# Residual gate's products placed in attention and in the branch projection, one PSUM pool from the groups on, and the forms' buffers opened before the keys

## The chip, the cores and the metric

The kernel runs on one core of a Trainium2 chip. The metric is device time in microseconds (us) of one execution; each figure is the median of several runs. PE is the matrix engine (PEld its weight loads), DVE the vector engine, ACT the scalar engine (activation functions, copies), POOL the GpSimd engine, SP the engine that does nothing here but start loads. SP, ACT and POOL start transfers; all transfers share the core's 16 DMA engines.

## The reference, cut to what matters

```python
# SEQ=512 tokens, D=2048, CTX=256, 12 query heads on 4 key heads of 128, FNet width 512
shift, scale, gate = split(silu(c) @ w_ada + b_ada, 3)         # modulation; gate is a row of 2048
h  = rmsnorm(x, norm_g) * (1 + scale) + shift
hc = rmsnorm(ctx, norm_g) * (1 + scale_c) + shift_c
kc, vc = heads(hc @ w_in[:, K and V]);  kc = rmsnorm(kc)
p  = h @ w_in                                                   # q, k, v, z_a, u_b, z_b, g_a, g_b
q, k = rope(rmsnorm(q)), rope(rmsnorm(k))
attn = softmax(q @ [k; kc].T) @ [v; vc]
y_a  = (attn * silu(z_a)) @ w_pa
y_b  = (real(fft2(u_b per group)) * silu(z_b)) @ w_pb
y    = (sigmoid(g_a) * y_a + sigmoid(g_b) * y_b) @ w_out
out  = rmsnorm(x + gate * y, final_g)
```

The *residual gate* is the row `gate`: a product of `silu(c)` with 2048 columns of `w_ada`. It is wanted only at the very end, where the output is scaled.

## The kernel before

Matmuls are made in pairs of numbers: each fp32 operand is split into a high and a low part (`split_from`: ACT rounds the high part, L141, DVE takes the difference for the low part, L142), and `mm3` issues three matmuls, high by high, high by low, low by high (L268, L269, L270). So every weight piece of 128x1024 that comes in by DMA costs ACT about 1.05 us and DVE about 1.22 us before PE can use it.

The program goes through these stages; Python loops write them out, and a scheduler then sets the order of the instructions on each engine, by priorities and by when it expects operands. The order on an engine is fixed afterwards: an instruction that waits holds all behind it on that engine, the DMA issues of that engine included.

- Start (0 to about 205 us): modulation, the pieces `u_b` for the FNet, and the FNet itself. `form_row(j)` builds row j of the operand combinations ("forms" S3, Z5, S2, S4 ..., since the big projection is a Strassen-Winograd product of 2x2 blocks) and stores it to a scratch tensor `f_d` in HBM; POOL issues this store (L558). The tile `f` has one buffer, so the next row's first write (L551) waits for the store.
- Keys and values (about 205 to 315 us), weights `w_kv`, then seven groups of about 81 us: groups 0 to 2 give q and z (stored to `qz_d`), groups 3 to 6 give the sigmoid gates g_a, g_b (`gate_done`, stored to `g_d` by ACT). A group runs Strassen pieces P2 ... Q5, P7, Q3, Q4; each has weight pieces `wr<-in_w_g` loaded by SP, and accumulates in PSUM tiles `x` and `y`. The forms come back from `f_d` by SP (`s<-f_d`, L313) into tiles of the pool `fm` and are split on arrival.
- Attention (about 895 to 1097 us): 48 steps (12 heads x 4 row blocks), in each step `scores(i)` (matmuls, DVE maximum L1068, ACT Exp), `turn(i-1)` (PE transposes of the weights, split into `pth` and `ptl`), every second step `values`, and between them a `filler`: the matmuls of w_pb. PSUM has a pool of its own here (`psa`).
- Branch projection (about 1097 to 1230 us): four column blocks (`CHUNKS`) x six pieces of w_pa (`wr<-in_w_pab`), 24 matmuls each, in another PSUM pool; POOL loads `g_d` back (`s<-g_d`), DVE multiplies by the gates (L1215, L1219, L1220), PE transposes the merged rows, ACT copies them out (L1162).
- Output groups (about 1230 to 1395 us), weights w_o, then the final norm. `load_rows` (issued by ACT, L1240) reads the gate row back from the scratch tensor `gs`.

The residual gate before: in groups 3 to 6 a list of jobs asks for one piece of the transposed w_ada (`ask_gate(q)`, 512 KB, SP, `wr<-in_w_gate`) and two jobs later DVE multiplies it by the row silu(c) and sums along the row (`use_gate`, L955, result in `gparts[:, q]`). There are 32 pieces; the row silu(c) is loaded and made twice (`crow`: L941 ACT, L942 DVE), one half for 16 pieces. The pieces use the same raw buffers `wr` as the weights. After group 6 DVE adds the parts (L1011, L1012: `gcol`, 128x16) and POOL stores them to `gs` (L1013) in 4-byte pieces.

Of the kernel before, what the change touches and what calls it, by code (L numbers as in the profile page):

```python
# [93 lines left out]
def block_kernel(ctx, tc, xT, ctxT, x, c_row, w_ss, w_gate, vecs, qkg, rope, dft_c, dft_s,  # L94
# [223 lines left out]
    def tiles(key):  # L318

        new = [take((1024,), F32R, fm) for _ in range(2)]  # L320
        kept.setdefault(key, []).extend(new)
        return new
# [223 lines left out]
    def form_row(j):  # L546

        f = pap.tile([P, 4, 256], F32, tag="f4", bufs=1, name=uid("f4"))
        v = pap.tile([P, 2, 256], F32, tag="f2", bufs=1, name=uid("f2"))
        for kb, t in ((j, f[:, 0:2, :]), (j + 8, v)):  # L550
            nc.vector.tensor_tensor(t, *(w[kb].bitcast(F32).rearrange("p (i c) -> p i c", i=2) for w in (hhi, hlo)),  # L551
                                    op=ALU.add)
# [4 lines left out]
        nc.vector.tensor_tensor(s4, v[:, 0, :], s2, op=ALU.subtract)  # L557
        nc.gpsimd.dma_start(f_d[:, :, j, :].rearrange("f p c -> p f c"), f)  # L558

    work = start_work()  # L560
    done = 0
    for kb in range(KK):
# [20 lines left out]
    form_row(6)  # L583
    form_row(7)
    pa.close()
# [89 lines left out]
    chain += [rp.tile([P, 1024], F32, name=f"R{pc}") for pc in range(4)]  # L675
    raw_pools.append((rp, 2, "raw", 2))
    cp, cpp = region("cp", "right")
# [88 lines left out]
    pss.close()  # L766
    fm = ctx.enter_context(tc.tile_pool(name="fm", bufs=1, reuse_waits="tile"))
# [4 lines left out]
    psum = [psp]  # L772
    rows4 = lambda hi, lo: [(hi[:, j, :], lo[:, j, :]) for j in range(4)]

    def split_form(src, pool):
        hi, lo = slot(pool, (4, 256), F32R), slot(pool, (4, 256), F32R)
        split_from(src, hi, lo)
        return rows4(hi, lo)

    def pair(tag):  # L780
        return psum[-1].tile([P, 2, 512], F32, tag=tag, bufs=2, name=uid(tag))

# [11 lines left out]
    class Banks:  # L794


        def __init__(self):
            self.b = [pair("y") for _ in range(2)]

# [79 lines left out]


    for i, f in enumerate(FORMS):
        forms[f] = [None] * 8
        for h in range(2):
            if (i, h) < (3, 1):
                whole[f, h] = slot(fm, (4, 256))

    ropeq = qzp.tile([P, 2, 4, HD], F32, name="ropeq")
# [45 lines left out]

    crow = None

    def silu_of_row(half):

        row = gvp.tile([P, 1024], F32, tag="crow", bufs=1, name=uid("crow"))
        nc.scalar.dma_start(row, c_row[:, 1024 * half : 1024 * half + 1024].broadcast_to([P, 1024]))
        e = flat(new_ev())  # L940
        nc.scalar.activation(e, row, ACT.Tanh, scale=0.5)  # L941
        nc.vector.scalar_tensor_tensor(row, e, 1.0, row, op0=ALU.add, op1=ALU.mult)  # L942
        return row

# [4 lines left out]
    def use_gate(q):  # L949

        if not any(e.key == ("gate", q) for e in ahead):
            jobs.insert(0, lambda: use_gate(q))
            return
        w = get_aside(("gate", q))
        nc.vector.scalar_tensor_tensor(w, w, 0.5, crow, op0=ALU.mult, op1=ALU.mult, accum_out=gparts[:, q : q + 1])  # L955

    def finish_jobs():
        for _ in range(16):
            load_more()
            job()  # L960
        assert not jobs

# [17 lines left out]
    for g in range(NQZ + NGATE):  # L980
        if g == NQZ:
            qzs.close()
            gvs, gvp = region("gvp", "right", reuse_waits="tile")
            raw_pools.append((gvp, 1, "raw", 1))
        if g in (NQZ, NQZ + 2):
            finish_jobs()
            crow = silu_of_row((g - NQZ) // 2)
            for q in range(8 * (g - NQZ), 8 * (g - NQZ) + KK):
                jobs += [lambda q=q: ask_gate(q), lambda: None, lambda q=q: use_gate(q)]
        group = Group(g, forms, new_ev, qz_done if g < NQZ else gate_done, {"a": "x", "b": "y", "c": "x"})  # L990
        for name in ONE_GROUP:
# [4 lines left out]
            if (g, name) == (0, "Q5"):  # L996
                hl_pools += range(MORE_HL)
                rotations()
            elif (g, name) == (LAST, "Q3"):
                finish_jobs()  # L1000
                raw_pools.pop()

                free += [(fm, f"s{i % KK}") for i in range(7, 7 + KK)]
# [8 lines left out]
    nc.vector.tensor_tensor(gcol, gcol, bada[:, 2 * KK :], op=ALU.add)  # L1012
    nc.gpsimd.dma_start(gs.rearrange("k p -> p k"), gcol)  # L1013
    gvs.close()
    evs.close()
    psg.close()

# [3 lines left out]
    ats_, atp = region("atp", "right", reuse_waits="tile")  # L1021
    psa_, psa = region("psa", None, space=PSUM, reuse_waits="tile")
    b1 = lambda: psa.tile([P, 512], F32, tag="b1", bufs=1, name=uid("pb"))
    ybs, S = {}, {}

    def filler():
# [5 lines left out]
        for n, j in enumerate(CHUNKS):  # L1032
            w = [get(("pab", j, pc)) for pc in BRANCH_B]
            for t in range(4):
                if t % 2 == 0:

                    y = chain[2 * n + t // 2].rearrange("p (t c) -> p t c", t=2) if n < 2 else take((2, 512))
                    ybs[j, t // 2] = y
                acc = psa.tile([P, 512], F32, tag="acc", bufs=1, name=uid("pf"))
                s = slice(t * P, t * P + P)  # L1040
# [18 lines left out]
    def scores(i):  # L1059
# [3 lines left out]
        qh, ql = qs[h][:, 0, s], qs[h][:, 1, s]  # L1063
        sc = psa.tile([P, 1024], F32, tag="sc", bufs=2, name=uid("sc"))
        for a, b in ((0, 512), (512, 768)):
# [12 lines left out]
    def turn(i):  # L1078
        p = probs.pop(i)
        tp = psa.tile([P, 1024], F32, tag="tp", bufs=1, name=uid("tp"))  # L1080
        for k in range(KT):
# [7 lines left out]
    def values(half):  # L1089
# [13 lines left out]
        if second:  # L1103
# [4 lines left out]
            if h % GQ == GQ - 1:  # L1108
                give(*kept.pop(h // GQ))

    filled = 0
# [21 lines left out]
    fill(1)  # L1133
    ats_.close()
    psa_.close()
    psum.append(ctx.enter_context(tc.tile_pool(name="psm", bufs=1, space=PSUM, reuse_waits="tile")))

# [4 lines left out]
    def load_gate(which, half, j):  # L1142
        t = take((2, 512), pool=gp)
        nc.gpsimd.dma_start(t, g_d[which, half, j].rearrange("p (t c) -> p t c", t=2))
        return t

    raws, merged, mf, comb = {}, {}, {n: [None] * 8 for n in ("A11", "A12", "A22") + FORMS}, {}
    held = {}
# [44 lines left out]
    for n, j in enumerate(CHUNKS):  # L1193
# [7 lines left out]
        ga = [load_gate(0, h, j) for h in range(2)]  # L1201
        accs = [pair("yx"[n % 2]) for _ in range(2)]
        for pc in BRANCH_A:
            wh, wl = get(("pab", j, pc))
            sh, sl = S[pc]
            for t in range(4):
                s = slice(t * P, (t + 1) * P)
                for k in range(2):
                    mm3(accs[t // 2][:, t % 2, :], sh[:, k, s], sl[:, k, s], wh[:, k, :], wl[:, k, :],
                        pc == 0 and k == 0, pc == BRANCH_A[-1] and k == 1)  # L1210
            if pc:
                job()
            if pc in (2, 3):
                y = ybs[j, pc - 2]
                nc.vector.tensor_tensor(y, gb[pc - 2], y, op=ALU.mult)  # L1215
                give(gb[pc - 2])
                gb[pc - 2] = y
        for h in range(2):
# [3 lines left out]
        give(*ga)  # L1222
        turned = [lambda j=j, i=i, n=n: turn_merged(j, i, "yx"[n % 2]) for i in range(2)]
        if n == 3:
# [151 lines left out]
    hl_pools.append(more)  # L1376
    out_group = Group(8, mf, new_o, lambda half, c, v, t: out_done(half, 2 + c, v, t), {"a": "y", "b": "x", "c": "y"})
    for name in OUT_GROUP:
        out_group.run(name)

    last_group = Group(9, mf, new_o, out_done, {"a": "y", "b": "x", "c": "y"}, last)
    for name in ONE_GROUP:
# [91 lines left out]
```

## Time and the profile before

| what | value |
|---|---|
| median of 3 runs | 1409.72 us (1404.27, 1409.72, 1410.72) |
| profiled execution | 1406.93 us, span 1405.2 us |
| PE busy | 1338.1 us, 95% |
| DVE busy | 981.5 us, 70% |
| ACT busy | 672.7 us, 48% |
| POOL busy | 142.3 us, 10% |
| moved | 265.73 MB read from HBM, 27.27 MB written |
| largest weight streams | `wr<-in_w_g` 112 loads, `wr<-in_w_gate` 32, `wr<-in_w_pab` 32, 512 KB each |

How to read it: PE does nearly all of the span, so time can come only from PE's idle stretches, from the stretches in which PE's clock was granted at half (the column PEclk of the windows view is the mean granted clock; 0.90 over 35 us means 3.5 us of full-speed work lost), or from fewer matmuls. A row of a group reads: line, engine, operation, written tile <- read tiles, shapes, count, then busy us and mean ns of one, then the engine's idle time just before these instructions and what ended it.

### The profile page before, as it was taken

Reading aid. Unit: us, or ns where it says so; the run is one execution under the profiler, and the core shown is the slowest. Engines: PE = TensorE matmul, PEld = TensorE weight load, DVE = VectorE, ACT = ScalarE, POOL = GpSimd, SP = SyncE. Lnnn points to the kernel's source line nnn. Section 1 sums busy time; section 2 is a strip of 40 time slices with the busy share of each in tenths; the row PEclk is TensorE's granted clock in tenths of the full one; section 3 lists DMA queues with packets and bytes.
Section 4 is the critical chain, followed back from the end, with each engine's and each line's share of the span. In section 5 each row is a group of like instructions: output and inputs, shape, how many; then the busy total and the mean of one; then the engine's idle time right before and its main releaser. Section 6 shows DMA issues by size and latency. Waiting matters only on the chain. (4 is left out here: it accounts for less than half of the span.)

```text
span 1405.2 us, 17732 instructions
## 1 busy us (share of the span) xinstructions
PE 1338.1 (95%) x6664; PEld 1084.1 (77%) x6664; DVE 981.5 (70%) x1266; ACT 672.7 (48%) x1036; POOL 142.3 (10%) x196
## 2 busy tenths in 40 slices
PE   7999899999999999999999996999999999999996
PEld 4667688787888888787777875888888788887885
DVE  4778695767887878786676864666766355578777
ACT  5322163446555555444354442677666223354544
POOL 1111000112111111101000010000000100010100
PEclk9999999999999999999999998999999999999998
DMA  9898466559888888897889998420311654378983
GB/s 384 341 371 313 150 229 211 183 180 319 236 226 217 200 245 210 242 349 214 260 258 247 302 253 192 154 87 26 96 46 35 220 180 135 106 153 217 229 224 135
DMA packets 90085, 294.16 MB, mean 209 GB/s; under 512 B 9232, under 2 KB 22032, under 8 KB 85648
## 3 DMA queue, kind: packets, MB, share of 16 engines
q1 hardware_dynamic: 51264, 178.46, 38.1%
q0 software_dynamic: 22320, 95.44, 27.0%
q10 hardware_dynamic: 16416, 19.14, 4.1%
q8 instruction: 52, 0.85, 0.2%
q14 instruction: 33, 0.27, 0.1%
HBM read 265.73 MB, written 27.27 MB: 209 GB/s over the span
## 5 line engine op out<-in xcount | busy, mean ns | idle before, releaser
L141 ACT ACTIVATE whi<-wr 128x1024 fp32r<-128x1024 f32 (+1 forms) x151 | 158.0, 1047 | 261.7 <-PE y L270 89.2
L142 DVE TENSOR_TENSOR wlo<-wr,whi 128x1024 fp32r<-128x1024 f32 (+1 forms) x151 | 181.4, 1206 | 100.2 <-ACT whi L141 99.8
L269 PE MATMUL x<-wlo,s 128*128 128x512 f32 x448 | 177.8, 397 | 8.2 <-DVE wlo L142 8.2
L268 PE MATMUL x<-whi,s 128*128 128x512 f32 x448 | 177.8, 397 | 4.5 <-ACT ev L837 3.4
L270 PE MATMUL x<-whi,s 128*128 128x512 f32 x448 | 176.5, 394 | 0.0
L268 PE MATMUL y<-whi,s 128*128 128x512 f32 x404 | 160.4, 397 | 10.5 <-ACT whi L141 7.3
L269 PE MATMUL y<-wlo,s 128*128 128x512 f32 x404 | 160.5, 397 | 6.1 <-DVE wlo L142 6.0
L270 PE MATMUL y<-whi,s 128*128 128x512 f32 x404 | 159.5, 395 | 0.0
L141 ACT ACTIVATE whi<-R 128x1024 fp32r<-128x1024 f32 x96 | 100.9, 1058 | 105.4 <-PE x L270 59.8
L142 DVE TENSOR_TENSOR wlo<-R,whi 128x1024 fp32r<-128x1024 f32 x96 | 116.5, 1220 | 22.2 <-ACT whi L141 22.0
L269 PEld LDWEIGHTS x<-wlo,s 128*128 128x128 f32 x448 | 85.8, 192 | 28.4 <-DVE wlo L142 10.8
L268 PEld LDWEIGHTS x<-whi,s 128*128 128x128 f32 x448 | 85.5, 191 | 23.3 <-ACT ev L837 3.8
L270 PEld LDWEIGHTS x<-whi,s 128*128 128x128 f32 x448 | 85.8, 192 | 18.0
L268 PEld LDWEIGHTS y<-whi,s 128*128 128x128 f32 x404 | 77.1, 191 | 27.8 <-ACT whi L141 7.7
L269 PEld LDWEIGHTS y<-wlo,s 128*128 128x128 f32 x404 | 77.1, 191 | 25.5 <-DVE wlo L142 9.8
L224 POOL DMA_DIRECT2D R<-in_w_g x56 | 48.8, 872 | 435.5 <-DVE wlo L142 263.7
L270 PEld LDWEIGHTS y<-whi,s 128*128 128x128 f32 x404 | 77.1, 191 | 16.7 <-DVE s L142 0.8
L141 ACT ACTIVATE s<-wr 128x512 fp32r<-128x512 f32 (+2 forms) x82 | 55.1, 690 | 55.7 <-DMA wr<-b_d 12.9
L215 DVE TENSOR_TENSOR wr<-R,wr 128x1024 f32<-128x1024 f32 x36 | 43.9, 1221 | 46.5 <-DMA wr<-in_w_g 28.3
L269 PE MATMUL x<-s,s 128*128 128x512 f32 x192 | 74.7, 389 | 0.0
L270 PE MATMUL x<-s,s 128*128 128x512 f32 x192 | 74.7, 389 | 0.0
L141 ACT ACTIVATE s<-R 128x512 fp32r<-128x512 f32 (+1 forms) x89 | 57.4, 661 | 30.8 <-PE x L270 17.4
(299 smaller groups left out, 2892.9 us busy)
## 6 DMA issues: line engine op xcount, KB each, us to landing
wr<-in_w_g SPq DMA_DIRECT2D x112, 512.0 KB, 4.8
wa<-in_w_ss POOLq DMA_DIRECT2D x28, 1024.0 KB, 9.0
R<-in_w_g POOLq DMA_DIRECT2D x56, 512.0 KB, 8.3
wr<-in_w_gate SPq DMA_DIRECT2D x32, 512.0 KB, 4.7
wr<-in_w_pab SPq DMA_DIRECT2D x32, 512.0 KB, 3.9
R<-in_w_g SPq DMA_DIRECT2D x28, 512.0 KB, 5.3
wr<-in_w_kv SPq DMA_DIRECT2D x24, 512.0 KB, 4.0
wr<-in_w_o SPq DMA_DIRECT2D x24, 512.0 KB, 5.1
```

Source lines behind the costliest of these rows:

```text
L141: nc.scalar.activation(hi, src, ACT.Copy)
L142: return nc.vector.tensor_tensor(lo, src, hi.bitcast(F32), op=ALU.subtract)
L215: nc.vector.tensor_tensor(src, chain[e.pc], src, op=ALU.subtract)
L224: nc.gpsimd.dma_start(chain[e.pc], e.nxt, accum_op=ALU.add)
L268: nc.tensor.matmul(o, ah, bh, start=start, stop=False, skip_group_check=cont)
L269: nc.tensor.matmul(o, ah, bl, start=False, stop=False, skip_group_check=cont)
L270: nc.tensor.matmul(o, al, bh, start=False, stop=stop, skip_group_check=cont)
```

## The change

Nothing of what is computed changes, and the counts of matmuls, of loads and of the gate's 32 products are the same. It has these parts:

1. The store of a form row goes from POOL to ACT (`keep_row`), and is written one block later, before the next row is built.
2. The pool `fm` is opened before the keys, so the six first form loads have free buffers there; the later forms take slots from `fm` and a second pool `fm2`.
3. In groups 3 to 6 no gate pieces are loaded or multiplied any more.
4. In attention, every third step uses one gate piece and asks for the next (16 in all); in the branch projection one piece per step of `m` (16 more); only then are `gcol` and its store to `gs` issued. `crow` now lies in a buffer of the pool `rp` (`raw1`).
5. PSUM has one pool (`psp`, tags x, y0, y1) from the groups to the end; attention's tiles `sc`, `tp`, `acc`, `b1` are taken from it. The first six pieces of the branch projection (`products`, a generator) start in attention's last three steps, and the filler runs three pieces further ahead.

```diff
-        nc.gpsimd.dma_start(f_d[:, :, j, :].rearrange("f p c -> p f c"), f)
+        made.append((j, f))
+    def keep_row():
+        j, f = made.pop()
+        nc.scalar.dma_start(f_d[:, :, j, :].rearrange("f p c -> p f c"), f)
...
+        if kb > 10:
+            keep_row()
         if kb >= 10:
             form_row(kb - 10)
...
+    fm = ctx.enter_context(tc.tile_pool(name="fm", bufs=1, reuse_waits="tile"))
+    for i, f in enumerate(FORMS):
+        for h in range(2):
+            if (i, h) < (3, 1):
+                whole[f, h] = slot(fm, (4, 256))
...
-    psg, psp = region("psg", None, space=PSUM, reuse_waits="tile")
+    psp = ctx.enter_context(tc.tile_pool(name="psp", bufs=1, space=PSUM, reuse_waits="tile"))
...
     def use_gate(q):
         w = get_aside(("gate", q))
-        nc.vector.scalar_tensor_tensor(w, w, 0.5, crow, op0=ALU.mult, op1=ALU.mult, accum_out=gparts[:, q : q + 1])
+        nc.vector.scalar_tensor_tensor(w, w, 0.5, crow[0], op0=ALU.mult, op1=ALU.mult, accum_out=gparts[:, q : q + 1])
...
-        if g in (NQZ, NQZ + 2):
-            finish_jobs()
-            crow = silu_of_row((g - NQZ) // 2)
-            for q in range(8 * (g - NQZ), 8 * (g - NQZ) + KK):
-                jobs += [lambda q=q: ask_gate(q), lambda: None, lambda q=q: use_gate(q)]
...
-    nc.vector.tensor_tensor(gcol, gparts[:, :KK], gparts[:, KK:], op=ALU.add)
-    nc.vector.tensor_tensor(gcol, gcol, bada[:, 2 * KK :], op=ALU.add)
-    nc.gpsimd.dma_start(gs.rearrange("k p -> p k"), gcol)
...
     for i in range(NSTEP + 2):
...
+            if i == 4:
+                silu_of_row()
...
-        want = 60 * (i + 1) // NSTEP if i < NSTEP else 64
+        want = min(3 + 61 * (i + 1) // NSTEP, 64)
...
+        if i % 3 == 2 and i < NSTEP:
+            if i > 2:
+                use_gate(i // 3 - 1)
+            ask_gate(i // 3)
...
+        if i == NSTEP - 1:
+            fill(1)
+            first_sums = [pair("x") for _ in range(2)]
+            first = products(CHUNKS[0], first_sums)
+        if i >= NSTEP - 1:
+            next(first)
+            next(first)
+    use_gate(KK - 1)
+    load_row(1)
+    silu_of_row()
...
+            m += 1
+            if 3 <= m < 19:
+                use_gate(KK + m - 3)
+            if m < 16:
+                ask_gate(KK + m)
+            if m == 19:
+                nc.vector.tensor_tensor(gcol, gparts[:, :KK], gparts[:, KK:], op=ALU.add)
+                nc.vector.tensor_tensor(gcol, gcol, bada[:, 2 * KK :], op=ALU.add)
+                nc.gpsimd.dma_start(gs.rearrange("k p -> p k"), gcol)
```

The scheduler turns this into the following orders (rows: line, operation, written tile <- read tiles; numbers behind a name tell buffers apart).

SP before, at the end of the keys' weights: the six form loads stand behind nine loads of the first group's weights.

```order
L177 DMA wr_2922<-in_w_g 128x1024
L177 DMA wr_3103<-in_w_g 128x1024
L177 DMA wr_2940<-in_w_g 128x1024
L313 DMA s_2787<-f_d 128x1024
L313 DMA s_2788<-f_d 128x1024
L313 DMA s_2789<-f_d 128x1024
L313 DMA s_2790<-f_d 128x1024
L313 DMA s_2791<-f_d 128x1024
L313 DMA s_2792<-f_d 128x1024
L177 DMA wr_2999<-in_w_g 128x1024
```

And SP after, at the beginning of the keys' weights:

```order
L706 DMA ct_2261<-in_ctxT 128x512
L313 DMA s_2024<-f_d 128x1024
L706 DMA ct_2295<-in_ctxT 128x512
L177 DMA wr_2338<-in_w_kv 128x1024
L313 DMA s_2025<-f_d 128x1024
L313 DMA s_2026<-f_d 128x1024
L177 DMA wr_2362<-in_w_kv 128x1024
L313 DMA s_2027<-f_d 128x1024
L177 DMA wr_2407<-in_w_kv 128x1024
L313 DMA s_2028<-f_d 128x1024
L313 DMA s_2029<-f_d 128x1024
L177 DMA wr_2431<-in_w_kv 128x1024
```

The form loads moved ahead of nearly all of `w_kv`.

DVE after, at the beginning of attention (L1079 is the maximum of a step's scores, L976 a gate product, `ptl` the low part of the turned weights, `s<-y` that of turned queries); before, no gate product stood here:

```order
L1079 TENSOR_REDUCE gain<-x_6722 128x1
L1079 TENSOR_REDUCE gain<-x_6750 128x1
L976 SCALAR_TENSOR_TENSOR wr_7135,gparts<-wr_7135,crow_6673 128x1024
L1082 RECIPROCAL gain<-gain 128x1 x2
L142 TENSOR_TENSOR ptl_6745<-tp_6737,pth_6744 128x6x128
L1079 TENSOR_REDUCE gain<-x_6781 128x1
L142 TENSOR_TENSOR s_6778<-y_6672,s_6778 128x512
L976 SCALAR_TENSOR_TENSOR wr_7293,gparts<-wr_7293,crow_6673 128x1024
L142 TENSOR_TENSOR ptl_6745<-tp_6765,pth_6744 128x6x128
L1082 RECIPROCAL gain<-gain 128x1
L1079 TENSOR_REDUCE gain<-x_6837 128x1
L1082 RECIPROCAL gain<-gain 128x1
```

Gate pieces g2 and g3 stand between the maxima of steps 2, 3 and 4; the load of g3 goes into the buffer that g2 leaves, and so on to g5.

ACT after, in the second column block of the branch projection (L1199 copies the turned rows out, L1282 is the read of the gate row from `gs`, `whi` a weight split); before, the read of `gs` stood in the fourth block, first issued at 1222.4 us:

```order
L141 ACTIVATE whi_9069<-wr_8988 128x1024
L1199 COPY s_9060<-x_9051 128x512
L1199 COPY s_9061<-x_9051 128x512
L1282 DMA s_9745<-gs 128x1024
L1199 COPY s_9060<-x_9097 128x512
L1199 COPY s_9061<-x_9097 128x512
L141 ACTIVATE whi_9113<-wr_9021 128x1024
```

The read of `gs` now stands ahead of `whi_9113`, the split of that block's sixth piece. DVE after, where the last products and the sums are:

```order
L142 TENSOR_TENSOR wlo_9024<-wr_8940,whi_9023 128x1024
L976 SCALAR_TENSOR_TENSOR wr_9393,gparts<-wr_9393,crow_8809 128x1024
L1247 TENSOR_TENSOR s_7955<-s_9225,s_7955 128x1024
L1247 TENSOR_TENSOR s_8491<-s_9477,s_8491 128x1024
L142 TENSOR_TENSOR wlo_9070<-wr_8988,whi_9069 128x1024
L976 SCALAR_TENSOR_TENSOR wr_9432,gparts<-wr_9432,crow_8809 128x1024
L1256 TENSOR_TENSOR gcol<-gparts 128x16
L1257 TENSOR_TENSOR gcol<-gcol,small 128x16
L142 TENSOR_TENSOR wlo_9114<-wr_9021,whi_9113 128x1024
```

The sums of the gate now stand here, three rows after the low part of the fifth piece of the second block; the store to `gs` on POOL follows them.

More of the change, by code (lines that the diff above doesn't have):

```diff
@@ L318, in tiles @@
     def tiles(key):
-        new = [take((1024,), F32R, fm) for _ in range(2)]
+        new = [take((1024,), F32R) for _ in range(2)]
         kept.setdefault(key, []).extend(new)
@@ L675, in block_kernel @@
     chain += [rp.tile([P, 1024], F32, name=f"R{pc}") for pc in range(4)]
-    raw_pools.append((rp, 2, "raw", 2))
+    raw_pools += [(rp, 1, f"raw{i}", 1) for i in range(2)]
+    fm = ctx.enter_context(tc.tile_pool(name="fm", bufs=1, reuse_waits="tile"))
[3 more added lines that the diff above has]
+                whole[f, h] = slot(fm, (4, 256))
     cp, cpp = region("cp", "right")
@@ L766, in block_kernel @@
     pss.close()
-    fm = ctx.enter_context(tc.tile_pool(name="fm", bufs=1, reuse_waits="tile"))
+    fm2 = ctx.enter_context(tc.tile_pool(name="fm2", bufs=1, reuse_waits="tile"))
+    fms = [fm2 if i >= 7 else p for i, p in enumerate([fm] * KK)]
+    turn_fm = [7]
     evs, evp = region("evp", "right", reuse_waits="tile")
@@ L797, in __init__ @@
         def __init__(self):
-            self.b = [pair("y") for _ in range(2)]
+            self.b = [pair("x") for _ in range(2)]
         def __getitem__(self, i):
@@ L932, in qz_done, with load_row, silu_of_row @@
                                 r[:, b])
[L934 to L943, printed above, removed]
+    crow = [None]
+    def load_row(half):
+        crow[0] = rp.tile([P, 1024], F32, tag="raw1", bufs=1, name=uid("crow"))
+        nc.scalar.dma_start(crow[0], c_row[:, 1024 * half : 1024 * half + 1024].broadcast_to([P, 1024]))
+    def silu_of_row():
+        e = take((1024,))
+        nc.scalar.activation(e, crow[0], ACT.Tanh, scale=0.5)
+        nc.vector.scalar_tensor_tensor(crow[0], e, 1.0, crow[0], op0=ALU.add, op1=ALU.mult)
+        give(e)
     def ask_gate(q):
@@ L1010, in block_kernel @@
             group.run(name)
-    nc.vector.tensor_tensor(gcol, gparts[:, :KK], gparts[:, KK:], op=ALU.add)
-    nc.vector.tensor_tensor(gcol, gcol, bada[:, 2 * KK :], op=ALU.add)
-    nc.gpsimd.dma_start(gs.rearrange("k p -> p k"), gcol)
     gvs.close()
     evs.close()
-    psg.close()
     free += [(hm, f"s{(9 + i) % KK}") for i in range(KK)]
     ats_, atp = region("atp", "right", reuse_waits="tile")
-    psa_, psa = region("psa", None, space=PSUM, reuse_waits="tile")
-    b1 = lambda: psa.tile([P, 512], F32, tag="b1", bufs=1, name=uid("pb"))
+    turned_y = last_y[0] % 2
+    both = pair("y")
+    fill_acc, b1 = both[:, 0, :], lambda: both[:, 1, :]
+    assert not any(p[0] is gvp or p[2] == "raw1" for e in ahead for p, _ in e.raws)
+    load_row(0)
     ybs, S = {}, {}
@@ L1109, in values, with products @@
                 give(*kept.pop(h // GQ))
+    def products(j, accs):
+        for pc in BRANCH_A:
+            wh, wl = get(("pab", j, pc))
+            sh, sl = S[pc]
+            for t in range(4):
+                s = slice(t * P, (t + 1) * P)
+                for k in range(2):
+                    mm3(accs[t // 2][:, t % 2, :], sh[:, k, s], sl[:, k, s], wh[:, k, :], wl[:, k, :],
+                        pc == 0 and k == 0, pc == BRANCH_A[-1] and k == 1)
+                yield pc, t
     filled = 0
@@ L1201, in block_kernel @@
         ga = [load_gate(0, h, j) for h in range(2)]
[L1202 to L1210, printed above, removed]
+        accs = [pair("xy"[n % 2]) for _ in range(2)] if n else first_sums
+        for pc, t in products(j, accs) if n else first:
+            if t < 3:
+                continue
             if pc:
                 job()
[L1213 to L1217, printed above, removed]
+            if pc > 3:
+                y = ybs[j, pc - 4]
+                nc.vector.tensor_tensor(y, gb[pc - 4], y, op=ALU.mult)
+                give(gb[pc - 4])
+                gb[pc - 4] = y
+            m += 1
[7 more added lines that the diff above has]
+                nc.gpsimd.dma_start(gs.rearrange("k p -> p k"), gcol)
+                raw_pools.append((rp, 1, "raw1", 1))
         for h in range(2):
@@ L1222, in block_kernel @@
         give(*ga)
-        turned = [lambda j=j, i=i, n=n: turn_merged(j, i, "yx"[n % 2]) for i in range(2)]
+        turned = [lambda j=j, i=i, n=n: turn_merged(j, i, "xy"[n % 2]) for i in range(2)]
         if n == 3:
```

57 lines of the change are left out of this document (28 added, 29 removed).

## The prediction

> **What bounds the kernel now.** I read the page's totals first, then the windows by stage, then PE's list of waits, then the rows around the longest of them.
>
> Totals and the windows by stage (stretch in us, its length, then busy time of PE, PEld, DVE, ACT and POOL with instruction counts, the mean granted clock, the DMA share, GB/s):
>
> ```profile
> span 1405.2 us, 17732 instructions
> PE 1338.1 (95%) x6664; PEld 1084.1 (77%) x6664; DVE 981.5 (70%) x1266; ACT 672.7 (48%) x1036; POOL 142.3 (10%) x196
> ...
> 140.00:205.00 65.00, 60.73 (x315) 48.23 (x314) 49.60 (x89) 25.39 (x39) 4.61 (x7) 0.95 0.57 187
> 315.00:350.00 35.00, 32.03 (x128) 25.38 (x127) 27.40 (x26) 22.30 (x25) 6.70 (x9) 0.90 1.00 325
> 350.00:560.00 210.00, 210.00 (x928) 173.96 (x927) 172.37 (x200) 114.59 (x216) 32.66 (x35) 1.00 0.84 222
> 560.00:595.00 35.00, 31.64 (x127) 25.66 (x127) 25.58 (x33) 16.25 (x20) 4.17 (x5) 0.90 0.90 239
> 595.00:840.00 245.00, 234.54 (x1017) 191.07 (x1017) 178.29 (x213) 111.14 (x138) 22.81 (x27) 0.99 0.90 270
> 840.00:895.00 55.00, 44.42 (x177) 35.12 (x176) 28.63 (x32) 21.28 (x24) 2.31 (x3) 0.88 0.80 206
> 895.00:1085.00 190.00, 185.60 (x1219) 159.35 (x1219) 121.73 (x194) 133.95 (x259) 4.25 (x8) 1.00 0.18 55
> 1085.00:1097.00 12.00, 6.98 (x45) 5.40 (x44) 7.23 (x8) 5.61 (x8) 0.53 (x1) 0.98 0.62 214
> 1097.00:1230.00 133.00, 133.00 (x616) 111.27 (x616) 69.14 (x59) 40.08 (x46) 8.82 (x16) 0.99 0.50 159
> ```
>
> PE is busy 1338 of 1405 us, so a change that keeps all matmuls can only win PE's idle time and the work lost at half clock (length times one less the clock). The reader is to see two kinds of stage. From 350 to 560, in the groups without gate pieces, PE is busy 210.00 of 210 us at full clock. From 560 to 895, where gate pieces are loaded and multiplied, it is idle in every stretch and the clock falls. Attention has DMA at 0.18 and DVE idle for 68 of 190 us; the branch projection has DMA at 0.50 and DVE idle for 64 of 133.
>
> PE's waits (engine and line, waited for; us in total, times, longest):
>
> ```profile
> PE x L269 <- DVE wlo L142: 8.2, 5, 2.7
> PE y L268 <- ACT whi L141: 7.3, 1, 7.3
> PE y L269 <- DVE wlo L142: 6.0, 6, 1.8
> PE pb L268 <- ACT s L463: 4.6, 2, 4.3
> PE tp L1082 <- DVE ptl L142: 3.8, 4, 1.9
> PE x L268 <- ACT ev L837: 3.4, 1, 3.4
> ```
>
> **Gain 1, the gate leaves groups 3 to 6.** What holds DVE's `wlo` there is DVE itself, standing for gate pieces, and the last gap comes from the store of the gate row (groups of instructions: busy and mean ns, then idle before and its releaser; then loads with KB each and us to landing; then timeline rows):
>
> ```profile
> L955 DVE SCALAR_TENSOR_TENSOR wr<-wr,crow 128x1024 f32<-128x1024 f32 x32 | 38.9, 1221 | 44.9 <-DMA wr<-in_w_gate 44.8
> L955 DVE DVE_READ_ACCUMULATOR wr<-wr,crow 128x1 f32 x32 | 2.6, 82 | 0.0
>   DMA wr<-in_w_gate: 44.8, 12
> ...
> wr<-in_w_gate SPq DMA_DIRECT2D x32, 512.0 KB, 4.7
> wr<-in_w_pab SPq DMA_DIRECT2D x32, 512.0 KB, 3.9
> wr<-b_d SPq DMA_DIRECT2D x2, 512.0 KB, 13.3
> gs<-gcol POOLq DMA_DIRECT2D x1, 8.0 KB, 14.7
> ...
> 855.16 1.23 POOL L1013 DMA_DIRECT2D gs<-gcol  x1 [16.95 <-DVE gcol L1012]
> 856.64 2.59 SPq L177 DMA_DIRECT2D wr<-b_d  x2
> 874.49 0.80 PE L268 MATMUL y<-whi,s 128*128 128x512 f32 x1 [7.32 <-ACT whi L141]
> ```
>
> A product costs DVE 1.221 + 0.082 = 1.30 us, 32 of them 41.7, and DVE stood another 44.8 us in 12 waits for the pieces. Without both, these groups have what groups 0 to 2 have, plus two raw buffers. Idle and clock by stretch: 560 to 595 lost 3.36 + 3.5; 595 to 840 lost 10.46 + 2.5; 840 to 895 lost 10.58 + 6.6. In the last one the loads of `b_d`, issued 1.5 us behind the store of `gs`, take 13.3 us, ACT waits for them and PE stands 7.32 us; the store goes away there. The sum is 37.0. I keep back 3 for loads that become late next (the forms and the group's own pieces, now first in SP's queue): 34, with 19 as the low end (only the 840 stretch and a tenth of the rest) and 37 as the high end.
>
> **Gain 2, the forms ahead of the keys.** Here 2.94 us of wait and the clock of 0.90 come from the six form loads behind weight loads at a DMA share of 1.00:
>
> ```profile
> s<-f_d SPq DMA_DIRECT2D x6, 512.0 KB, 13.0
> 328.84 0.79 PE L268 MATMUL y<-whi,s 128*128 128x512 f32 x1 [2.94 <-ACT s L141]
> ```
>
> With the loads some 20 SP rows earlier, in a stage of less traffic, they are long there. Idle 2.97 + clock 3.5 = 6.5; I take 6. The high bound is 6.5. What hides six loads in the keys' stage is the slack of `w_kv`; if that is gone, each costs at most the 1.6 us that 512 KB take at the 325 GB/s of 315 to 350, an estimate, thus 10 us and a loss of 3 on balance.
>
> **Gain 3, the store of a form row.** POOL issued it without delay (its queue was idle until DVE had the row), and L551 waited for the landing of some:
>
> ```profile
> L551 DVE TENSOR_TENSOR f<-s,s 128x512 f32<-128x512 f32 x16 | 11.0, 690 | 11.5 <-DMA f_d<-f 11.1
> L558 POOL DMA_DIRECT2D f_d<-f x8 | 6.2, 773 | 61.4 <-DVE f L557 59.3 <-DVE gain L537 2.1
> f_d<-f POOLq DMA_DIRECT2D x8, 512.0 KB, 4.2
> ```
>
> ACT issues later than POOL did, so L551 can wait longer; but POOL's other loads no longer stand behind DVE. PE's 4.3 us wait for L463 and the 0.95 clock in 140 to 205 (4.27 + 3.3) are the most that it can win, and as much again the most that it can lose. I take +1, near nothing, as the tile still has one buffer.
>
> **Gain 4, no PSUM border.** In 1085 to 1097 PE idles 5.02 us, since the last `ptl` are waited for with nothing else to run, and 0.2 + 1.3 us of clock go. Now matmuls of the first block stand between: 6.5 at most, 0 at least; I take 5. The 46 us of the four gains are 34 + 6 + 1 + 5.
>
> **Loss 1, gates at the start of attention.** The load of g2 needs the buffer that g0 leaves, g3 that of g2, g4 that of g3, g5 that of g4. So each turn costs a load of 3.9 us (as `wr<-in_w_pab`, in the same quiet stage) and a product of 1.3, and DVE can't overlap the turn with itself: 5.2 us, four turns 21. Before, DVE's maxima of these steps stood so:
>
> ```profile
> 894.87 1.81 DVE L1068 TENSOR_REDUCE gain<-sc 128x1 f32<-128x768 f32 x2
> ...
> 912.30 0.96 DVE L1068 TENSOR_REDUCE gain<-sc 128x1 f32<-128x768 f32 x1
> ```
>
> That is 17.4 us for the same six or seven maxima. DVE gets 4 to 6 us late; PE has two score tiles and the filler ahead, so between 0 and 9 us (4 plus two half-clock windows and more) reach it. I take 4. The other ten products stand between steps with their pieces loaded, 1.3 us each in idle DVE time: 1, between 0 and 3.
>
> **Loss 2, piece g17.** Its load starts when g16's product ends, at the end of attention; DVE waits some 3 us in front of the last `ptl` and a `wlo`. 0 to 5, I take 3.
>
> **Loss 3, the gate row's way to memory and back.** ACT issues the read of `gs` ahead of the split of the second block's sixth piece, and an engine's queue holds all behind. SP's list of waits shows a queue standing up to 12.1 us for a buffer:
>
> ```profile
> SPq L177 <- DVE wr L955: 99.4, 32, 12.1
> 1106.05 1.06 ACT L141 ACTIVATE whi<-wr 128x1024 fp32r<-128x1024 f32 x1 [3.99 <-PE y L270]
> 1111.49 1.06 ACT L141 ACTIVATE whi<-wr 128x1024 fp32r<-128x1024 f32 x1 [4.38 <-PE y L270]
> 1145.11 1.06 ACT L1162 COPY s<-y 128x512 f32<-128x512 f32 x2
> ```
>
> Count from the end of g16's product. PE needs that piece after the last steps of attention (7 us, the 6.98 busy of 1085 to 1097), six pieces of 5.44 us (1111.49 - 1106.05) of the first block, five of the second and two turnings of 0.9: 7 + 11 x 5.44 + 1.8 = 68.6. DVE's rows up to `gcol` are 15 products (19.5), 9 `wlo` (11.0 at 1.22), 7 + 4 multiplications (13.5 at 1.23) and small ones (3.9): 48; but the last `wlo` ahead waits for a piece that PE leaves at 7 + 8 x 5.44 = 50.5, so `gcol` is there at 54.5 at the earliest. If a third of the products wait for loads, 62. Store: 0.9 to its issue, 14.7 to landing, then ACT has its issue, two copies and the split, 3.4 us, then `wlo`. PE goes on at 54.5 + 20.2 = 74.7 or at 82.2, thus idles 6 or 13.5 us, and 1.7 to 5 us at half clock follow (in 840 to 895, gaps of 2.7 and 7.3 us were followed by 6.6 of lost clock). Between 8 and 19, I take 12; 0 if the store is quick. Losses: 4 + 1 + 3 + 12 = 20.
>
> **The sum.** 46 - 20 = 26 us. The profiled execution took 1406.93 (span and 1.7 around it), so 1381; it lies 2.8 us under the median of the runs, 1409.72, which would give 1384. I say 1382.
>
> **Two rules weighed.** The trace shows what a short gap does:
>
> ```profile
> 659.11 0.50 PE L269 MATMUL x<-wlo,s 128*128 128x512 f32 x1 [1.79 <-DVE wlo L142]
> 655.00:665.00 10.00, 8.21 (x30) 6.26 (x29) 6.37 (x6) 3.16 (x5) 0.00 (x0) 0.83 0.60 179
> ```
>
> A gap of 1.79 us was followed by 1.7 us lost to the clock (0.17 of 10). The Trainium skill, page "TensorE: Matmul & The Clock Gate", section "Why this matters for your kernels", advises against idle gaps over about 3 us only; by it losses 1 and 2 would cost no clock and the sum would be about 3 us better. The row decides against it. For the store of 8 KB the row is 14.7 us. The Trainium skill, page "DMA: Bandwidth & Descriptors", section "Anatomy of one DMA — SWDGE (gpsimd) path", gives 2.0 us plus bytes by 436 GB/s, thus 2.0 us here, an estimate; it would make the read harmless. The row speaks against that.
>
> **Rivals.** (A) The store is quick in the branch stage, where DMA is at 0.50 and not at 0.80. ACT must have the read off by 68.6 - 3.4 = 65.2, so the store may take 9.8 us if `gcol` is there at 54.5, and 2.3 if at 62; then loss 3 is 0: 1382 - 12 = 1370. Against it: 8 KB in 4-byte pieces is the same work wherever it stands. The fit of the Trainium skill's DMA page, named above, speaks for this rival. (B) The gaps of 560 to 840 stay, as they come from SP's queue at 0.90 DMA and not from gate pieces: 19.8 us of gain 1 less, 1402. Against: groups 0 to 2 run at 0.84 with none, and 16.8 MB less are moved. (C) Attention stalls more, each of the first six gates 2 us and the clock with it: 1382 + 11 = 1393. (D) Slower: DVE stands 3.7 us (44.8 / 12) for every one of the 32 pieces, since each load starts only when a product frees a buffer, and half of it reaches PE: 59 us in place of losses 1 and 2, 1382 + 51 = 1433. It decides from (46 - 12) / 32 = 1.06 us of PE a gate; against it, DVE has 68 and 64 us idle in the two stages. (E) Nothing stalls: 1382 - 20 = 1362.
>
> **Chances.** Forecast (1375 to 1391) 0.50; A 0.15; B 0.12; C 0.12; D 0.07; E 0.04. 0.5% is 7 us, about what can be told from no change: 1402.7 and 1416.8. Faster: the forecast, A, C, E and a third of B, 0.85; same: most of B, 0.08; slower: D, 0.07. The range leaves out D and part of E and B: 1362 to 1400.
>
> **What would show it.** Right: windows of 560 to 840 (shifted) at PE full and clock 1.00; no gap before attention; the six `s<-f_d` landing in under 8 us; an ACT gap of over 10 us in the branch stage ended by the store of `gs`, with a PE wait for `whi` behind it. Wrong: PE waits for `wlo` still in groups 3 to 6; an L976 row with idle before it of over 60 us; no ACT gap.

## The result

The changed kernel takes 1393.82 us (median of 4 runs, 1389.75 to 1396.97), the kernel before 1410.04 us; the ratio is 0.9892, with a 95% interval of 0.9853 to 0.9931. That is 16 us less, where 26 to 28 were forecast: the right direction and inside the range of 1362 to 1400, but the forecast of 1382 is 12 us too low, and the time lies just outside the 1375 to 1391 that were given a chance of one half. The profiled execution's span is 1390.1 us, 15 less than before.

The windows of the changed kernel by stage (columns as before):

```profile
130.00:200.00 70.00, 66.17 (x357) 51.43 (x356) 54.42 (x95) 25.37 (x38) 1.06 (x2) 0.98 0.60 198
200.00:310.00 110.00, 107.42 (x538) 89.81 (x537) 71.37 (x111) 44.43 (x66) 16.86 (x24) 0.98 0.69 229
310.00:550.00 240.00, 240.00 (x1059) 198.57 (x1058) 201.48 (x226) 137.06 (x238) 37.54 (x39) 1.00 0.84 228
550.00:855.00 305.00, 305.00 (x1354) 252.70 (x1353) 204.10 (x218) 155.28 (x194) 30.97 (x37) 1.00 0.83 228
855.00:1055.00 200.00, 186.25 (x1197) 158.74 (x1197) 136.35 (x218) 131.04 (x253) 4.23 (x8) 1.00 0.30 92
1055.00:1095.00 40.00, 39.76 (x202) 32.92 (x201) 27.97 (x38) 13.14 (x18) 5.26 (x10) 1.00 0.90 325
1095.00:1128.00 33.00, 30.65 (x143) 24.87 (x142) 22.61 (x28) 4.26 (x5) 3.31 (x5) 1.00 0.85 287
1128.00:1150.00 22.00, 8.53 (x26) 6.12 (x25) 8.21 (x7) 5.92 (x7) 0.00 (x0) 0.61 0.56 146
```

All seven groups (310 to 855) now run at 545.00 busy of 545 us and full clock. Attention is idle for 13.75 of 200 us, where before it was 4.40 of 190. And one hole is new, at 1128.

Where the time went is seen best by counting matmuls: both kernels issue 6664, in nearly the same order, so the start of the n-th in one trace is compared with the n-th in the other (in attention the order differs a little; at number 5400 it meets again). The border behind the groups is number 4020, since in the kernel before the half clock behind the groups' last gap, of 7.32 us, runs on to about number 4010.

| up to matmul | stage that ends there | changed minus before, us | of the stage |
|---|---|---|---|
| 1600 | start, FNet, most of the keys | +0.3 | +0.3 |
| 1800 | first group begins (form loads) | -6.2 | -6.5 |
| 4020 | groups | -43.6 | -37.4 |
| 5400 | attention | -36.4 | +7.2 |
| 5800 | branch projection | -16.8 | +19.6 |
| 6663 | output | -15.0 | +1.8 |

Each number compares one trace with one other. Where the code of a stage is the same, such counts still differ: at number 1600 the variants of the changed kernel with the same start lie 0.3 to 3.2 us behind the kernel before, and over attention the kernel before without gate pieces lies 2.2 us behind it.

So 44 us were won up to attention, more than the 41 forecast for gains 1 to 3, and 29 were given back, 20 of them in the branch projection. PE's first wait, ACT's wait and the timeline say how:

```profile
PE y L268 <- ACT whi L141: 13.0, 1, 13.0
...
ACT s L1199 <- DMA gs<-gcol: 27.0, 1, 27.0
...
gs<-gcol POOLq DMA_DIRECT2D x1, 8.0 KB, 13.8
...
1124.50 0.17 DVE L1257 TENSOR_TENSOR gcol<-gcol,small 128x16 f32<-128x16 f32 x1
1125.36 1.20 POOL L1258 DMA_DIRECT2D gs<-gcol  x1 [4.77 <-DVE gcol L1257]
1139.33 0.33 ACTq L1282 DMA_DIRECT2D s<-gs  x1
1139.69 1.07 ACT L1199 COPY s<-x 128x512 f32<-128x512 f32 x2 [27.04 <-DMA gs<-gcol]
1140.65 1.07 ACT L141 ACTIVATE whi<-wr 128x1024 fp32r<-128x1024 f32 x1
1141.78 0.79 PE L268 MATMUL y<-whi,s 128*128 128x512 f32 x1 [13.01 <-ACT whi L141]
```

ACT stood 27.0 us at the read of `gs`, until the store had landed; the weight split behind it came 13 us late. It is the chain of loss 3, row by row.

### The profile page after: what moved, and what is told of

Same layout as the page of the kernel before. It is cut to its first block, busy times and chain, and to the rows that moved or that the text cites. A ratio compares the mean times of both kernels' runs of the same rounds, so it can differ in the third digit from the quotient of the medians.

```text
span 1390.1 us, 17752 instructions
## 1 busy us (share of the span) xinstructions
PE 1329.1 (96%) x6664; PEld 1079.8 (78%) x6664; DVE 983.6 (71%) x1266; ACT 674.7 (49%) x1036; POOL 136.9 (10%) x188
## 5 line engine op out<-in xcount | busy, mean ns | idle before, releaser
L268 PE MATMUL y<-whi,s 128*128 128x512 f32 x440 | 176.5, 401 | 17.3 <-ACT whi L141 13.0
L269 PE MATMUL x<-wlo,s 128*128 128x512 f32 x476 | 185.8, 390 | 0.6 <-DVE wlo L142 0.5
L268 PE MATMUL x<-whi,s 128*128 128x512 f32 x476 | 186.1, 391 | 0.2 <-ACT s L863 0.2
L270 PE MATMUL x<-whi,s 128*128 128x512 f32 x476 | 185.5, 390 | 0.0
L269 PE MATMUL y<-wlo,s 128*128 128x512 f32 x440 | 173.0, 393 | 2.5 <-DVE wlo L142 2.5
L270 PE MATMUL y<-whi,s 128*128 128x512 f32 x440 | 172.6, 392 | 0.0
L268 PEld LDWEIGHTS y<-whi,s 128*128 128x128 f32 x440 | 83.3, 189 | 40.5 <-ACT whi L141 13.4
L268 PE MATMUL x<-s,s 128*128 128x512 f32 (+1 forms) x280 | 106.6, 381 | 5.1 <-ACT s L141 4.2
L269 PE MATMUL x<-s,s 128*128 128x512 f32 (+1 forms) x292 | 109.6, 375 | 0.0
L270 PE MATMUL x<-s,s 128*128 128x512 f32 (+1 forms) x292 | 109.4, 375 | 0.0
L269 PEld LDWEIGHTS x<-wlo,s 128*128 128x128 f32 x476 | 89.4, 188 | 19.8 <-DVE wlo L142 1.5
L268 PEld LDWEIGHTS x<-whi,s 128*128 128x128 f32 x476 | 89.4, 188 | 19.1 <-ACT s L863 0.5
L270 PEld LDWEIGHTS x<-whi,s 128*128 128x128 f32 x476 | 89.3, 188 | 18.7
L269 PEld LDWEIGHTS y<-wlo,s 128*128 128x128 f32 x440 | 83.2, 189 | 19.2 <-DVE wlo L142 4.1
L270 PEld LDWEIGHTS y<-whi,s 128*128 128x128 f32 x440 | 83.2, 189 | 17.6
L142 DVE TENSOR_TENSOR s<-wr,s 128x512 fp32r<-128x512 f32 (+2 forms) x82 | 61.2, 764 | 23.1 <-ACT s L141 22.6
```

The source lines that it names most:

```text
L142: return nc.vector.tensor_tensor(lo, src, hi.bitcast(F32), op=ALU.subtract)
L268: nc.tensor.matmul(o, ah, bh, start=start, stop=False, skip_group_check=cont)
L269: nc.tensor.matmul(o, ah, bl, start=False, stop=False, skip_group_check=cont)
L270: nc.tensor.matmul(o, al, bh, start=False, stop=stop, skip_group_check=cont)
```

## The experiments

Each edit is made on the kernel named with it. "The POOL variant" is the first experiment's kernel. Times are medians beside runs of the kernel before in the same session (1410.7, 1409.6, 1410.7 us).

**The read of `gs` issued by POOL.**

```diff
-            nc.scalar.dma_start(l[g], src...)
+            (nc.gpsimd if l is gates else nc.scalar).dma_start(l[g], src...)
```

> The changed kernel, with the read of the gate row from gs issued by POOL instead of ACT. Theory (ACT's queue is held by the read until the store has landed): PE's gap of 13.0 us and the half clock behind it go, no ACT idle of 27 us ended by the store; 16 us less than the changed kernel, about 1378 us. Rival (the branch stage is short of weights, since DMA is at 0.85 to 0.90 with gate pieces in it): PE stops at the same place for whi or wlo, at most 5 us less, about 1389.

1376.39 us, ratio 0.9754 (0.9714 to 0.9794). The gap at the same place is gone (longest PE gap of the stage 1.89 us), though the store takes as long, 14.4 us. The branch stage gives back 4.1 us instead of 19.6, so the read in ACT's queue cost 15.5: the gap of 13.0 and the half clock behind it. The theory holds; what POOL holds behind the read is not needed soon.

**The gate row stored in pieces of 64 bytes.** (The row's elements come out in another order.)

```diff
-                nc.gpsimd.dma_start(gs.rearrange("k p -> p k"), gcol)
+                nc.gpsimd.dma_start(gs.rearrange("k (a j) -> (k a) j", j=KK), gcol)
```

> The changed kernel with the gate row stored to gs in 128 pieces of 64 bytes instead of 2048 of 4 bytes (the order of its elements is then another). Theory (the number of pieces sets the store's 13.8 us): it lands in 2 to 5 us, ACT's wait falls from 27 to about 18 us and PE's gap from 13.0 to about 4 us; 10 us less, about 1383. Rival (the store waits behind other transfers at a DMA share of 0.85): landing over 11 us, the gap stays over 10 us, 1391 or more.

1386.82 us, ratio 0.9820 (0.9788 to 0.9852).

```profile
gs<-gcol POOLq DMA_DIRECT2D x1, 8.0 KB, 6.0
...
PE y L268 <- ACT whi L141: 3.7, 1, 3.7
```

The same 8 KB land in 6.0 us instead of 13.8, and PE's gap falls from 13.0 to 3.7. The branch stage gives back 10.0 us instead of 19.6. Rival A thus had the right mechanism (a quick store nearly frees ACT) and the wrong place: the branch stage doesn't make it quick, larger pieces do.

**The kernel before without gate pieces.** (The 32 products, their loads and the row silu(c) are left out.)

```diff
...
-            crow = silu_of_row((g - NQZ) // 2)
-            for q in range(8 * (g - NQZ), 8 * (g - NQZ) + KK):
-                jobs += [lambda q=q: ask_gate(q), lambda: None, lambda q=q: use_gate(q)]
```

> The kernel before without the 32 gate pieces in groups 3 to 6 (loads and products and the row silu(c) are left out, the store of gs stays). Theory (gate pieces make DVE and raw buffers late there): PE is busy without a gap from 330 to the start of attention, clock 1.00; 36 us less than before, about 1374. Rival (SP's queue and DMA at 0.9 make the gaps): the gaps of 560 to 840 stay, 12 to 17 us less, about 1395.

1382.00 us, ratio 0.9782 (0.9749 to 0.9815).

```profile
345.00:855.00 510.00, 509.77 (x2248) 421.71 (x2248) 372.38 (x408) 265.96 (x399) 64.12 (x70) 1.00 0.83 227
```

PE is busy 509.77 of 510 us; from matmul 1800 to 4020 this kernel gains 36.9 us, as the change does (37.4). Rival B is dead. The total is less since 9 us are lost in the first 50 us: with nothing to wait for, the store of `gs` is issued at 3.0 us, among the first loads, and PE waits 15.2 us there in three pieces instead of 8.5 in one. That the store is the cause was not tried by itself.

**No gate pieces in attention.** (16 products and their loads and the first half row are left out.)

```diff
-    load_row(0)
...
-            if i == 4:
-                silu_of_row()
...
-        if i % 3 == 2 and i < NSTEP:
-            if i > 2:
-                use_gate(i // 3 - 1)
-            ask_gate(i // 3)
...
-    use_gate(KK - 1)
```

> The changed kernel without the 16 gate pieces of attention (their loads, products and the first row silu(c) are left out; the 16 of the branch projection stay). Theory (the products hold DVE in turns of 5 us and cost PE idle time): PE's idle time in attention, 13.8 us in the 200 us from 855, falls to about 5, DVE's maxima of steps 0 to 6 span 17 us instead of 22; 9 us less, about 1385. Rival (the new order of filler, scores and PSUM buffers makes these gaps): idle stays above 11 us, 1391 or more. In both the gap of 13 us in the branch projection stays.

1385.54 us, ratio 0.9810 (0.9777 to 0.9842). The time is what the theory expected, the idle time is not: 9.24 us of the 200, between the two. Nor did DVE's maxima answer as expected: the first seven span 21.3 us here and 20.3 in the changed kernel, where 17 and 22 were expected.

```profile
855.00:1055.00 200.00, 190.76 (x1231) 163.13 (x1229) 125.47 (x196) 134.19 (x259) 4.25 (x8) 1.00 0.18 57
```

By matmuls, attention (4020 to 5400) gives back 1.2 us now, where the changed kernel gives back 7.2: the 16 products, with their loads, cost 6.1. The hole of the branch stage is smaller too (9.7 instead of 13.0 us).

Half of the 6.1 is lost at the turns at the beginning: by matmul 4280, at 889 us, the changed kernel has lost 3.0 us against this one. The turns are as forecast, 4.9 to 5.3 us a product, and behind each of four products a DVE row that PE needs comes late (rows of the changed kernel):

```profile
857.03 1.23 DVE L976 SCALAR_TENSOR_TENSOR wr<-wr,crow 128x1024 f32<-128x1024 f32 x1 [0.46 <-DMA wr<-in_w_gate]
859.43 0.85 PE L1093 MATMUL tp<-ident,s 128*128 128x128 f32 x6 [0.77 <-DVE ptl L142]
861.90 1.23 DVE L976 SCALAR_TENSOR_TENSOR wr<-wr,crow 128x1024 f32<-128x1024 f32 x1 [1.15 <-DMA wr<-in_w_gate]
864.06 0.39 PE L269 MATMUL y<-ptl,s 128*128 128x256 f32 x1 [0.78 <-DVE ptl L142]
867.24 1.23 DVE L976 SCALAR_TENSOR_TENSOR wr<-wr,crow 128x1024 f32<-128x1024 f32 x1 [1.02 <-DMA wr<-in_w_gate]
868.86 0.50 PE L268 MATMUL y<-whi,s 128*128 128x512 f32 x1 [0.59 <-DVE s L1113]
872.29 1.23 DVE L976 SCALAR_TENSOR_TENSOR wr<-wr,crow 128x1024 f32<-128x1024 f32 x1 [0.76 <-DMA wr<-in_w_gate]
874.51 0.39 PE L269 MATMUL y<-ptl,s 128*128 128x256 f32 x1 [0.54 <-DVE ptl L142]
```

These four gaps of PE make 2.7 us; without the products PE waits once in that time, for 0.97 us. The other 3 us are lost in small pieces up to about 1000 us.

**Part 2 alone on the kernel before** (fm ahead of the keys, fm2 for later forms; the edit is that of the diff).

> The kernel before with part 2 alone: pool fm opened ahead of the keys, the six form loads early, fm2 for the later forms. Theory (the form loads' wait at the first group goes, 2.9 us and 3.4 us of clock, and the keys' stage hides them but for a gap of 1 to 2 us): no PE gap at 326, 4 to 6 us less than before, about 1405. Rival (the loads only move their delay into the keys' stage): gaps there of 5 us or more, same time as before within 2 us.

1403.65 us, ratio 0.9951 (0.9930 to 0.9972). The gap at 326 is gone and the keys' stage has gaps of 0.90 and 1.05 us only. Gain 2 is real, about 6 us.

**Part 1 undone in the POOL variant.**

```diff
-        nc.scalar.dma_start(f_d[:, :, j, :].rearrange("f p c -> p f c"), f)
+        nc.gpsimd.dma_start(f_d[:, :, j, :].rearrange("f p c -> p f c"), f)
```

(issued at the end of `form_row`, as before)

> The variant whose gs read is issued by POOL, with part 1 undone: a form row is stored by POOL again, at once. Theory (the store's issuer is worth nothing: the gap near 166 us only changes place with one near 139 us): the same time as that variant within 2 us, 1376, with a gap of about 4 us near 166 or 170 again. Rival (ACT's store wins the 4 us gap and its clock): 1381 or more.

1378.35 us, ratio 0.9768 (0.9741 to 0.9796), 2 us above the POOL variant, whose interval it overlaps. The gap of before is back, and the one of the changed kernel is gone:

```profile
170.37 0.80 PE L268 MATMUL pb<-s,whi 128*128 128x512 f32 x1 [4.27 <-ACT s L463]
...
141.38 0.69 PE L484 MATMUL pd<-ident,ado 128*128 128x128 f32 x2 [3.80 <-ACT ado L481]
...
173.06 0.57 PE L268 MATMUL pb<-s,whi 128*128 128x512 f32 x1 [4.66 <-ACT s L463]
```

The rows are of the kernel before, the changed one and this one. Part 1 moves a 4 us gap 30 us forward and is worth nothing that these runs can tell.

**Products held to their step in attention** (on the POOL variant).

```diff
...
+            nc.vector.tensor_scalar(half, after, 0.0, 0.5, op0=ALU.mult, op1=ALU.add)
-        nc.vector.scalar_tensor_tensor(w, w, 0.5, crow[0], ...)
+        nc.vector.scalar_tensor_tensor(w, w, half, crow[0], ...)
...
-                use_gate(i // 3 - 1)
+                use_gate(i // 3 - 1, stats[:, 4 * (i % 4) + 2 : 4 * (i % 4) + 3])
```

> The variant whose gs read is issued by POOL, with each gate product of attention held until the step where the code has it: its factor 0.5 is a column made from that step's reciprocal (DVE TENSOR_SCALAR, 128x1), so that a piece has three steps to land. Theory (DVE's waits for pieces, 8.7 us in 11 waits, cost PE 6 us in attention): L976's waits for in_w_gate go and PE's idle time in the 200 us from 855 falls from 14.7 to about 10; 4 us less, about 1372. Rival (the products' own 1.3 us in DVE's queue cost it): idle time the same, 1376.

1379.41 us, ratio 0.9777 (0.9747 to 0.9808): no gain. DVE's waits for pieces are gone in attention (8.7 us in 11 waits in the changed kernel) and idle time there fell to 10.9 us, as expected, but a new gap stands at its end:

```profile
ACT s L965 <- DMA crow<-in_c_row: 4.7, 1, 4.7
...
1071.66 0.58 PE L268 MATMUL y<-pth,s 128*128 128x256 f32 x1 [3.77 <-ACT pth L141]
```

The second half of the row silu(c) goes into the buffer of the first, so its load waits for the last product of attention, ACT waits for the load, and `pth` stands behind ACT. It is loss 3's pattern again, an ACT instruction that waits for a transfer in front of work that PE needs.

**Held in the branch projection as well** (each product behind the low part of its own weight piece).

```diff
             wh, wl = get(("pab", j, pc))
+            last_lo[0] = wl[:, 0, 0:1]
...
-                use_gate(KK + m - 3)
+                use_gate(KK + m - 3, last_lo[0])
```

> As the paced variant, and in the branch projection each product is held behind the low part of its own piece (one product for each 5.4 us of PE). Theory (the 16 products and loads crowd into the first 45 us of the branch stage, with DMA at 0.85 and more, and cost PE about 4 us there beside the gs read): PE full through the stage, another 3 us less than the paced variant, about 1369. Rival (gcol is then ready 50 us later, and its store and read on POOL hold the loads of w_o behind them): a gap at the start of the output groups, 1375 or more.

1375.02 us, ratio 0.9742 (0.9715 to 0.9769). The branch stage gives back nothing any more (matmul 5400 to 5800, 0.04 us against 4.1), so those 4 us were the crowding of the 16 products; the gap at the end of attention, here 2.9 us, hides the gain. So the 1369 expected was not reached; but the rival's gap at the start of the output isn't there either (no wait of PE there is longer than the 1.10 us that the changed kernel has too).

**Held in the branch projection only** (the edit just shown, on the POOL variant, with attention's products as in the changed kernel).

> The variant whose gs read is issued by POOL, with the products paced in the branch projection only (attention's as in the changed kernel). Theory (pacing in attention wins 2 us there and loses them at its end, where ACT waits for the second row silu(c); pacing in the branch wins 4): no gap of 2.9 us at the end of attention, none in the branch stage; 1372, 4 less than the variant without pacing. Rival (the branch's 4 us and the end of attention are one loss that moves): 1376.

1372.83 us, ratio 0.9733 (0.9708 to 0.9758), as expected: neither gap is there.

**Held in both, the second half row in a buffer of its own.**

```diff
-    use_gate(KK - 1)
-    load_row(1)
-    silu_of_row()
+    use_gate(KK - 1)
+    crow[0] = rows_c[0]
```

(with `load_row(1)` ahead of `load_row(0)` into `raw0`, which no longer takes weights there, and `silu_of_row` at step 24)

> The variant paced in both stages, with the second half of the row silu(c) loaded at the beginning of attention into a buffer of its own (raw0, which then takes no weights), so that ACT doesn't wait for it at attention's end. Theory (ACT's 3.8 us wait for that row holds pth behind it and makes the gap of 2.9 us and a half-clock window): the gap goes; 4 us less than the variant paced in both, about 1371. Rival (DVE's or the values' chain is late there anyway): the gap stays over 2 us, 1375.

1366.12 us, ratio 0.9683 (0.9660 to 0.9705). It is the fastest of all, 3.2% under the kernel before.

```profile
855.00:1055.00 200.00, 191.14 (x1231) 163.54 (x1230) 146.69 (x244) 134.67 (x261) 4.23 (x8) 1.00 0.30 95
1055.00:1150.00 95.00, 95.00 (x460) 79.57 (x460) 67.25 (x83) 29.05 (x35) 7.90 (x15) 1.00 0.80 278
```

Attention with the gate is idle for 8.86 us, as little as without it (9.24), and the branch stage is full. It is 5 us better than expected: some 4 us were won inside attention too (matmul 4200 to 5200), and whether the buffer taken from the weights or the early second row does that stays open.

## Why the prediction was right or wrong

The direction was right, and so were the mechanisms of gains 1 and 2 and of losses 1 and 3. Gain 4 failed, and loss 3 was taken too small.

- Gain 1, forecast 34, at most 37: 37.4 in the change, 36.9 with the gate pieces simply left out. Nothing became late next, so the 3 us kept back for that were not needed.
- Gain 2, forecast 6: 6.5 at the first group, 6 in the run of part 2 alone. The keys' stage hid the loads but for one gap of 1.81 us and its clock window, part of the start's scatter.
- Gain 3, forecast 1: nothing that shows above the scatter of the start. The gap changed its place.
- Gain 4, forecast 5: this step failed. Without gates in attention the change loses 1.2 us between matmul 4020 and 5400, where it should have won the 6.5 that the end gaps had cost; that is nothing, within the scatter. The gaps at the end are gone, but 9.24 us of idle time stand inside attention where 4.40 stood: the idle time moved from the end into the steps. Of the new order's parts (PSUM tags, filler ahead, first block between) none was tried alone.
- Loss 1, forecast 5 (4 for the turns, 1 for the other ten products): 6.1. The turns cost 3.0, by the wait that was forecast; the others cost 3.1, and no clock was lost. Loss 2, forecast 3: the product of g17 waited 0.41 us for its piece.
- Loss 3, forecast 12, range 8 to 19: this term was mis-sized. The count from the end of g16's product (1060.7) was close: PE came to the piece after 68.1 us (68.6 forecast), `gcol` was there after 64.0 (54.5 to 62, so later than the late end), the store took 13.8 (14.7), PE went on after 81.1 (82.2 at the late end). I took a value in the middle where the late end came true; the read cost 15.5, and the crowding of products and loads in that stage, which has no term in the sum, 4.1 more. Together 19.6.
- Output, no term: +1.8.

The misses add up: loss 3 19.6 instead of 12 (7.6 worse), attention with its end 7.2 lost instead of 3 (gain 4 less losses 1 and 2; 4.2 worse), output 1.8 worse, gains 1 to 3 2.6 better: 26 - 7.6 - 4.2 - 1.8 + 2.6 = 15.0, what the traces show.

Rival C had named 1393, but that it hit the time is luck: it put 2 us on each of the first six gates and clock lost with them, and the turns cost 3.0 us in all and no clock; most of the miss lies in the branch stage. Rival D needed 1.06 us of PE for a gate; the runs show 0.4 in attention (6.1 / 16) and 0.3 in the branch stage (4.1 / 16).

On the two rules. The clock: in the changed kernel's keys' stage stands this gap, and one window of 3.4 us at half clock behind it.

```profile
242.76 0.50 PE L269 MATMUL pd<-wlo,s 128*128 128x512 f32 x1 [1.81 <-DVE wlo L142]
...
239.90:243.30 3.40, 1.58 (x7) 1.03 (x6) 2.61 (x5) 1.85 (x3) 0.00 (x0) 1.00 0.80 278
243.30:246.70 3.40, 3.40 (x9) 2.65 (x8) 3.40 (x8) 0.96 (x3) 0.00 (x0) 0.50 0.90 249
```

The Trainium skill's page "TensorE: Matmul & The Clock Gate" (section "Why this matters for your kernels") warns of gaps over about 3 us only; behind this gap of 1.81 us the clock was halved. No clock was lost in attention, whose gaps are 1.1 us at most. But the length of the gap does not decide alone, as two others show:

```profile
39.80 0.44 PE L484 MATMUL pd<-ident,ado 128*128 128x128 f32 x2 [1.79 <-ACT ado L481]
...
1099.99 0.50 PE L269 MATMUL y<-wlo,s 128*128 128x512 f32 x1 [1.89 <-DVE wlo L142]
```

Behind these two, of the changed kernel and of the POOL variant, the clock stayed full. What differs is their place on a grid. Within each of the twelve traces all changes of the clock lie whole multiples of 3.41 us apart, and each trace can be cut into stretches on that grid. Of the stretches at full clock, all 33 in which PE idled for more than 1.8 us were followed by half clock, none of the 76 with 1.0 to 1.6 us, and 3 of the 12 between (idle time by the profile, from 16 us on). The gap of 1.81 us fell into one stretch, the first of the two windows above; the borders of the grid split the other two into 0.5 + 1.3 and 0.8 + 1.1 us. So in these runs the limit is about half a stretch of idle time, and where the grid lies differs from trace to trace.

The store: the fit of the Trainium skill's page "DMA: Bandwidth & Descriptors" (section "Anatomy of one DMA — SWDGE (gpsimd) path") gives 2.0 us for these 8 KB, an estimate. In pieces of 4 bytes it took 13.8, and 10.7 to 17.2 over the eleven runs that have it so; in pieces of 64 it took 6.0. The measurement decides, and the row of before had said so.

## What to carry to other kernels

Ask of every transfer what stands behind its issue on the issuing engine, and who needs that; a read-back of something just stored belongs on a queue whose next work is far off. A product moved into an idle stage is cheap only if its place is fixed by the work around it: where the scheduler places it as soon as it thinks the data is there, it waits for the data and crowds the queue. And when a chain can be timed from two ends, take the late end if each of its terms is bounded by a measured row.

## What the runs showed that was not expected

The same 8 KB took 13.8 us in 2048 pieces and 6.0 us in 128, both from POOL in the branch stage. Leaving work out made the kernel before lose 9 us at its start, probably because a store that had been late was then issued at 3.0 us. And of the 17 us at half clock around the 13 us gap, most fell on the gap itself, so that the clock cost 2.8 us there (half of the 5.6 in which PE ran) and not 8.5. Counting length times one less the clock, as the prediction does, takes idle time for lost clock as well.
